# Hyena and attention step on one core: the filter spectrum's odd classes with three real products, the skip weight in the filter's first tap

## Chip, cores and metric

The kernel runs on one core of a Trainium2 chip. The metric is the device time of one execution in microseconds. Three runs of the kernel before took 884.54, 884.93 and 885.29 us; the median is 884.93 us. The engines are named as the profile names them: PE is TensorE (PEld its weight loads), DVE is VectorE, ACT is ScalarE, POOL is GpSimd, and SP issues most of the DMA transfers.

## The reference

One layer of a hybrid backbone works on 128 context tokens and 512 latent tokens, model width 1024. After an adaptive modulation one projection gives a gated long convolution (Hyena) and an attention with their gates; both are merged, projected, and normalised. The change touches the long convolution:

```python
def hyena_filters(L, ...):
    hf = jnp.sin(f_freq[0] * (z @ f_w1 + f_b1))
    hf = jnp.sin(f_freq[1] * (hf @ f_w2 + f_b2))
    hf = (hf @ f_w3).astype(jnp.float32).reshape(L, 2, D_HYENA)
    decay = jnp.exp(-t * jnp.abs(deltas)) + DECAY_SHIFT
    hf = hf * decay[:, None, :]
    return hf[:, 0], hf[:, 1]

def hyena_long_conv(v_h, x1, x0, h_fwd, h_bwd, d_bias):
    L = v_h.shape[1]
    u = v_h * x1
    filt_full = jnp.concatenate([h_fwd, jnp.zeros_like(h_fwd[:1]), h_bwd[:0:-1]], axis=0)
    n = 2 * L
    uf = jnp.fft.rfft(u.astype(jnp.float32), n=n, axis=1)
    ff = jnp.fft.rfft(filt_full, n=n, axis=0)
    y = jnp.fft.irfft(uf * ff[None], n=n, axis=1)[:, :L].astype(u.dtype)
    return (y + u * d_bias) * x0
```

The result of the convolution is then multiplied by `silu(g_h)` and goes into the merging projections.

## The kernel before

Channels lie on the 128 partitions, the 640 tokens on the free axis: 128 of the context, then 512 latent ones in blocks of 64 (8 grid rows by 8 columns, rolled by one block). Every large product is made of three matmuls: the operands are split into a high part (type fp32r, written by ACT) and a low part (the rest, written by DVE), and high x high, high x low and low x high are accumulated in PSUM. `split` (L100 to L102) makes such a pair, `mm3` (L155 to L158) the three matmuls, `accumulate` (L163 to L171) the projections.

The 1024 channels of the long convolution are worked through in four quarters of 256, two row tiles of 128 each. For each quarter these generators yield their work in steps:

- `quarter_head` projects the tiles of u and x1, runs the short convolution on them (`conv_tile`, L530) and multiplies them (L569).
- `quarter_tail` projects x0 and the gate g_h, and writes gate times x0 into a row tile yh (`gapped_product`, L523, which also brings the tokens from grid order into block order).
- `filter_spectrum` (L431) makes the filter's transform. The 512 latent taps are four time classes (every fourth tap, classes 0 to 3), the 128 context taps are class 4. For a class, `src` (L450) multiplies the hidden layer by the last filter weights (tile fl), takes the decay (sd, L459) and splits (sh, sl, L462). Its two halves of 256 columns are the sum and the difference of the forward and the backward filter. A shifted cosine and sine transform (tables dftH, dftL) follows per class, and the classes are combined into ten rows F of a quarter. Classes 1 and 3 go into the PSUM tiles fc and fd in eight groups of three matmuls (L488 to L493), for half of which the table of class 3 is negated (ndH, ndL, made at L413), and four 512-wide DVE operations combine them with the even classes (L497 to L500).
- L441 to L448 compute, with a matmul on the hidden layer's first column (fz), the backward filter's first tap, and subtract it from the skip weight: `hyd`.
- `long_conv` transforms u by the same tables (tiles ut, c_X, s_X, p_X) and multiplies it by F (L638 to L646). `long_conv_back` transforms back (yb), transposes (yp for the context, y for the latent tokens), adds u times hyd (L689, L698) and calls `gate_conv`, which multiplies the result into yh and sends yh to DRAM.

Tiles live in pools with a fixed number of buffers per tag; a tile waits for its buffer. PSUM has eight banks: four for the projections (tag mm, two per projection tile), four for all else (tag aux). `weave` (L68) mixes a main generator (projections) with a side generator (convolution and filter) in a fixed ratio, and `braid` (L706) alternates two side generators: while quarter q is transformed back, the filter of quarter q + 1 is made. In these stages (L724 to L729) only SP's early loads and a few table operations keep the written order; the other instructions are put into an order for each engine at build time, by a planner that follows the written order as its priority and simulates when each is ready (L1555). From the attention on (L1254), and in the prologue, PE's order is the written one.

The last quarter's convolution is woven with the first queries, keys and values (L1200); behind it `attention_setup` gives the convolution's memory to the attention.

Of the kernel before, what the change touches and what calls it, by code (L numbers as in the profile page):

```python
# [36 lines left out]
    (("convw", 96), ("hyd", 8), ("ident", 128)),  # L37
# [8 lines left out]
def tile_hyena_natten_step(ctx: ExitStack, tc: tile.TileContext, a, o):  # L46
# [3 lines left out]
    def f(ap):  # L50
        return ap.bitcast(F32)
# [181 lines left out]
    def hidden_layers():  # L233
        hf1 = temp("u", "hf1", 4)[:64]
# [19 lines left out]
    def prologue():  # L254
# [61 lines left out]
        for k in range(NK):  # L316
# [5 lines left out]
            row_ = hwa.tile([P, 2 * P], F32, tag="fb", bufs=2, name=f"row{k}")  # L322
# [13 lines left out]
            if k == 0:  # L336
                load_pack(1)
                out["zemb"] = temp("u", "zemb", 4)[:33]
# [53 lines left out]
    ndH = hyc.tile([P, 2, P], F32R, tag="ndH", name="ndH")  # L392
    ndL = hyc.tile([P, 2, P], F32R, tag="ndL", name="ndL")
# [9 lines left out]
    def dft_consts():  # L403
# [8 lines left out]
        for nd, src in ((ndH, dftH), (ndL, dftL)):  # L412
            nc.scalar.activation(nd[:], f(src[:, 0, 3]), AF.Copy, scale=-1.0)  # L413
# [17 lines left out]
    def filter_spectrum(q):  # L431
        if q not in pre:
            load_filter(q)
        w3 = pre[q]
        w3h = hwa.tile([P, 512], F32R, tag="w3h", name=f"w3h_{q}")
        w3l = hwa.tile([P, 512], F32R, tag="w3l", name=f"w3l_{q}")
        w3s = hwa.tile([P, 2, 256], F32, tag="fb", bufs=2, name=f"w3s_{q}")
# [3 lines left out]
        pb0 = aux(f"fz{q}")  # L441
        for i in range(2):
            nc.tensor.matmul(
                pb0[:, i : i + 1], w3[:, 256 + P * i : 384 + P * i], f(hid[:, 0:1]),
                start=True, stop=True, skip_group_check=True,
            )
# [3 lines left out]
        def src(cls):  # L450
# [7 lines left out]
            sd = hwa.tile([P, 2, 256], F32, tag="fb", bufs=2, name=f"sd{q}_{cls}")  # L458
            nc.vector.tensor_tensor(sd[:], two(ps[:]), dec[:].unsqueeze(1).to_broadcast([P, 2, 256]), op=ALU.mult)  # L459
            sh = hw.tile([P, 2, 256], F32R, tag="shl", bufs=4, name=f"sh{q}_{cls}")  # L460
            sl = hw.tile([P, 2, 256], F32R, tag="shl", bufs=4, name=f"sl{q}_{cls}")
            split(sh[:], sl[:], sd[:])  # L462
            return (sh[:, 0], sl[:, 0]), (sh[:, 1], sl[:, 1])

        s0 = src(0)
# [7 lines left out]
        s2 = src(2)  # L473
# [6 lines left out]
        pc = pd = None  # L480
        for cls in (1, 3):
            cs, ds = src(cls)
            yield
            first = cls == 1
            if first:
                pc = aux(f"fc{q}")
                pd = aux(f"fd{q}")
            for dst, i, (sh, sl), neg, lead in (  # L488
                (pc[:, :256], 0, cs, False, True), (pc[:, 256:], 1, ds, False, False),
                (pd[:, :256], 1, cs, not first, True), (pd[:, 256:], 0, ds, not first, False),  # L490
            ):
# [5 lines left out]
        nc.vector.tensor_tensor(x[:, 0:6:5], x[:, 1:7:5], two(pc[:]), op=ALU.add)  # L497
        nc.vector.tensor_tensor(x[:, 1:7:5], x[:, 1:7:5], two(pc[:]), op=ALU.subtract)
        nc.vector.tensor_tensor(x[:, 2:9:6], x[:, 3:8:4], two(pd[:]), op=ALU.add)
        nc.vector.tensor_tensor(x[:, 3:8:4], x[:, 3:8:4], two(pd[:]), op=ALU.subtract)  # L500
        yield
        pp = aux(f"fp{q}")
# [53 lines left out]
    def quarter_head(q):  # L556
        us = []
        out[f"u{q}"] = us
        for i in range(2):
            n = 2 * q + i  # L560
            u = hw.tile([P, NG + 1], F32, tag="u", bufs=4, name=f"u{n}")
# [11 lines left out]
    half_done = set()  # L573

    def gate_conv(n):
        if n in half_done:
            gapped_product(out["yh"][n], out[f"u{n // 2}"][n % 2])
            nc.sync.dma_start(yh_d[n], out["yh"][n][:])
        half_done.add(n)

    def quarter_tail(q):
        yh = out["yh"]
        for i in range(2):
# [7 lines left out]
            gate_conv(n)  # L591
# [57 lines left out]
    def long_conv_back(q):  # L649
        us, ident, hyd, R, W = out[f"u{q}"], out["ident"], out[f"hyd{q}"], out[f"R{q}"], out[f"W{q}"]  # L650
# [18 lines left out]
        for g, rs_ in enumerate(((0, 2), (1, 3), (4,))):  # L669
# [13 lines left out]
            yield  # L683
        outp = aux(f"yp{q}")
        for i in range(2):
            nc.tensor.transpose(outp[:, i * P : i * P + P], yp[:, i * P : i * P + P], ident)
        for i in range(2):
            up = us[i][:, :LP]
            nc.vector.scalar_tensor_tensor(  # L689
                up, up, hyd[:, i : i + 1], outp[:, i * P : i * P + P], op0=ALU.mult, op1=ALU.add  # L690
            )
        for i in range(2):
            n = 2 * q + i
            oy = aux(f"y{n}")
            for j, r in enumerate((0, 2, 1, 3)):
                nc.tensor.transpose(oy[:, r * P : r * P + P], ye[:, j, i * P : i * P + P], ident)
            uv = us[i][:, GAP:NG].rearrange("p (m r) -> p r m", r=4)
            nc.vector.scalar_tensor_tensor(  # L698
                uv, uv, hyd[:, i : i + 1], oy[:].rearrange("p (r m) -> p r m", r=4), op0=ALU.mult, op1=ALU.add
            )  # L700
            gate_conv(n)
# [728 lines left out]
def _host_constants():  # L1430
    f32 = np.float32
    zs, decs = [], []
    for L in (LS, LP):
# [7 lines left out]
        if L == LS:  # L1441
            zs += [z[r::4] for r in range(4)]
# [121 lines left out]
```

## Time and profile before

| | |
|---|---|
| median of three runs | 884.93 us (884.54 to 885.29) |
| span of the profiled execution, first to last instruction | 883.0 us |
| median of the runs less this span | 1.9 us |
| PE, PEld, DVE, ACT, POOL busy | 871.0, 843.5, 632.7, 429.5, 128.8 us |
| bytes moved | 129.07 MB, 146 GB/s |

The profile gives, of the profiled execution, the span alone; what lies around it is taken as the difference to the median of the runs. By stage: the prologue (modulation, first weights, hidden layers of the filter) runs to about 46 us, the four quarters of the long convolution with their projections to about 386 us, the attention with the remaining projections to about 705 us, the merging and output projections to the end. PE's rows name the tile that is written and the tiles that are read; a matmul's weight load has a row of its own under PEld. A row of a group ends with the busy time, the mean duration in ns, and the idle time of the engine just before; a row of the timeline begins with the start and the duration in us.

### The profile page before, as it was taken

To read this page: it belongs to the slowest core of one execution; us is meant where nothing else is said; L and a number is where in the kernel's file an instruction comes from. 1 tells how busy PE (TensorE), PEld (TensorE's weight loads), DVE (VectorE), ACT (ScalarE), POOL (GpSimd) and SP (SyncE) were. 2 spreads that over 40 slices of the span, in tenths; PEclk is the share of its full clock that TensorE was granted. 3 is DMA by queue.
4 is the path that set the end of the run, shared out by engine and by line. 5 is a ranking of instruction groups with operands and counts; after the bars stand their busy time and mean duration, and the time that the engine had idled before them with its cause. 6 is when DMAs were issued, how large, how long until landed. Compare 5 with 4: busy or idle time off the path is not lost.

```text
span 883.0 us, 16773 instructions
## 1 busy us (share of the span) xinstructions
PE 871.0 (99%) x6522; PEld 843.5 (96%) x6522; DVE 632.7 (72%) x1247; ACT 429.5 (49%) x919; POOL 128.8 (15%) x130
## 2 busy tenths in 40 slices
PE   8999999999999999999999999999999999999996
PEld 7899999999999999999999999999999999999885
DVE  5576693795668478699787567865788567676656
ACT  4486454655545432356665465555666632243200
POOL 1111010010101000024423222222222200000000
PEclk9999999999999999999999999999999999999999
DMA  9976666565656231253525153433252478545511
GB/s 325 401 164 148 134 136 126 132 140 118 168 112 142 70 108 55 72 195 105 164 80 169 55 152 100 142 105 122 80 181 83 132 285 283 181 152 198 214 64 55
DMA packets 54986, 129.07 MB, mean 146 GB/s; under 512 B 8283, under 2 KB 24283, under 8 KB 54908
## 3 DMA queue, kind: packets, MB, share of 16 engines
q1 hardware_dynamic: 45260, 107.62, 37.1%
q0 software_dynamic: 4032, 14.68, 10.2%
q10 hardware_dynamic: 5616, 5.70, 1.9%
q8 instruction: 51, 0.84, 0.4%
q14 instruction: 27, 0.22, 0.1%
HBM read 113.83 MB, written 14.16 MB: 145 GB/s over the span
## 4 chain that ended last, share of the span: by engine, by line
PE 96%; DMA 3%; DVE 1%; SPq 0%; issue 0%; DVEq 0%
PE mm L168 37%; PE sp L1125 23%; PE mm L182 6%; PE out L1391 6%; PE v L821 5%; PE pt L918 3%; PE s L925 2%; PE s L878 2%; DMA ada<-wada 2%; PE ve L833 1%; DMA xt<-xT 1%; PE yb L158 1%; PE yb L156 1%; PE fl L453 1%; PE yb L157 1%; PE ut L601 1%
## 5 line engine op out<-in xcount | busy, mean ns | idle before, releaser
L1125 PE MATMUL sp<-t,wb 128*128 128x320 f32 x768 | 120.6, 310 | 0.0
L1125 PEld LDWEIGHTS sp<-t,wb 128*128 128x128 f32 x768 | 113.8, 188 | 0.5 <-issue 0.5
L168 PE MATMUL mm<-hL,wh 128*128 128x320 f32 x480 | 113.8, 312 | 0.0
L168 PE MATMUL mm<-hH,wh 128*128 128x320 f32 x480 | 113.3, 312 | 0.3 <-ACT hH L365 0.3
L168 PE MATMUL mm<-hH,wl 128*128 128x320 f32 x480 | 111.4, 310 | 0.0
L1125 PE MATMUL sp<-hH,wb 128*128 128x320 f32 x384 | 93.2, 313 | 0.0
L168 PEld LDWEIGHTS mm<-hH,wh 128*128 128x128 f32 x480 | 80.5, 188 | 2.2 <-issue 1.2
L168 PEld LDWEIGHTS mm<-hL,wh 128*128 128x128 f32 x480 | 81.0, 188 | 1.2 <-DVE hL L373 0.4
L168 PEld LDWEIGHTS mm<-hH,wl 128*128 128x128 f32 x480 | 80.6, 188 | 0.3
L1125 PEld LDWEIGHTS sp<-hH,wb 128*128 128x128 f32 x384 | 66.1, 188 | 1.9 <-issue 1.9
L900 POOL TENSOR_SCALAR p<-p,sm 128x384 f32<-128x384 f32 x32 | 46.5, 1462 | 111.8 <-DVE sm L899 98.1
L101 ACT ACTIVATE wh<-raw 128x1024 fp32r<-128x1024 f32 x31 | 32.8, 1059 | 59.2 <-PE mm L168 23.8
L1125 PE MATMUL sp<-hL,wb 128*128 128x320 f32 x192 | 59.3, 309 | 0.0
L148 POOL DMA_DIRECT2D wl<-wall x28 | 24.3, 869 | 226.6 <-ACT wl L147 159.3
L102 DVE TENSOR_TENSOR wb<-s,wb 128x512 fp32r<-128x512 f32 x64 | 44.0, 701 | 15.8 <-ACT wb L101 15.7
L101 ACT ACTIVATE wb<-s 128x512 fp32r<-128x512 f32 x64 | 39.1, 629 | 27.7 <-DVE s L1090 21.5
L101 ACT ACTIVATE wb<-raw 128x512 fp32r<-128x512 f32 x48 | 30.1, 628 | 34.1 <-PE sp L1125 22.0
L102 DVE TENSOR_TENSOR wl<-raw,wh 128x1024 fp32r<-128x1024 f32 x31 | 37.9, 1221 | 12.0 <-ACT wh L101 11.9
L149 ACT ACTIVATE wh<-raw 128x1024 fp32r<-128x1024 f32 x28 | 29.7, 1060 | 33.1 <-PE mm L168 33.0
L1391 PE MATMUL out<-woh,yhs 128*128 128x512 f32 (+1 forms) x176 | 45.5, 372 | 0.0
L900 POOL TENSOR_SCALAR edge<-edge,sm 128x320 f32<-128x320 f32 x32 | 42.5, 1339 | 1.9 <-DVE sm L899 1.9
L168 PE MATMUL mm<-yhs,wh 128*128 128x320 f32 x224 | 41.9, 309 | 0.0
(364 smaller groups left out, 2160.5 us busy)
## 6 DMA issues: line engine op xcount, KB each, us to landing
raw<-wall SPq DMA_DIRECT2D x93, 512.0 KB, 3.6
wl<-wall POOLq DMA_DIRECT2D x28, 512.0 KB, 5.7
ada<-wada SPq DMA_DIRECT2D x16, 512.0 KB, 6.7
tm<-bias SPq DMA_DIRECT2D x16, 512.0 KB, 4.9
gate<-wgate SPq DMA_DIRECT2D x8, 512.0 KB, 4.0
wo<-wall SPq DMA_DIRECT2D x8, 512.0 KB, 4.5
xt<-xT SPq DMA_DIRECT2D x8, 320.0 KB, 7.0
dec<-decay SPq DMA_DIRECT2D x20, 128.0 KB, 5.1
```

What stands on the lines that cost most here:

```text
L101: hi = nc.scalar.activation(dst_h, src, AF.Copy)
L102: return hi, (eng or nc.vector).tensor_tensor(dst_l, src, f(dst_h), op=ALU.subtract)
L148: nc.gpsimd.dma_start(wl, a["wall"][i], accum_op=ALU.add)
L149: nc.scalar.activation(wh, raw[:], AF.Copy)
L168: nc.tensor.matmul(ps[hf][:, :HALF], wt[k], x[:, hf * HALF : (hf + 1) * HALF], start=(i == 0 and k == 0), stop=(i == lead[2] and k == NK - ...
L182: nc.tensor.matmul(p[:, :HALF], w[i // 2][k], (hH, hL)[i % 2][:, k, cs], start=n == 0, stop=n == len(steps) - 1, skip_group_check=True,)
L821: nc.tensor.matmul(ps[t // 2][:, t % 2 * 256 : t % 2 * 256 + 256], x[:, k, P * t : P * t + P], wk, start=first and t % 2 == 0, stop=last, ...
L878: nc.tensor.matmul(dst[h], x[rows(h), qs], y[rows(h), ks], start=i == 0, stop=i == 2, skip_group_check=True)
L900: nc.gpsimd.tensor_scalar_mul(pv, pv, sm[:, 2:3])
L918: nc.tensor.transpose(pt[:, i * P : i * P + P], x, ident)
L1125: nc.tensor.matmul(dst, wk, x(xi, k), start=j < 4 and k == 0 and i == 0, stop=k == 3 and i == 2, skip_group_check=True,)
L1391: ins = nc.tensor.matmul(dst, m[k][:, c0 : c0 + P], w[:, c : c + n], start=(first and k == 0), stop=(last and k == 5), skip_group_check=True,)
```

## The change

- **Class 3 reversed.** The host now lays out the hidden layer's input and the decay of time class 3 in reverse order. The reversed class's cosine transform is then, up to an alternating sign by frequency, the sine transform of class 1, and its sine transform the cosine of class 1. The two odd classes together have the form of a complex product, which is computed with three real products: the cosine of class 1 on the sum of both classes' taps (into fc, both column halves), and two tables, sine minus and sine plus cosine (`gs`, split into gsH and gsL), on the one and the other class. ACT copies the common product out of fc (tile t) before the second products are accumulated on it; DVE subtracts it from fd. The alternating sign is a per-partition factor (`sgn`), applied by `turn` where the rows of F are made: eight 256-wide DVE operations in place of four 512-wide ones. The negated tables go.
- **Skip weight.** hyd, the matmul on the first column and the additions of u times hyd go. A row `skip` (one partition, 256 columns) is loaded per quarter and brought into the first tap (partition 0) of classes 0 and 4 by three small DVE operations.
- **Gating.** `long_conv_back` multiplies the transposed result, read from PSUM, straight into yh: one operation for the context, three for the latent tokens, whose order is changed on the way. As yh must hold gate times x0 by then, the generator yields until `quarter_tail` has written it (`opened`); u is not needed after its transform, and has three buffers instead of four. The tag fb has three instead of two.

```diff
-    ndH = hyc.tile([P, 2, P], F32R, tag="ndH", name="ndH")
-    ndL = hyc.tile([P, 2, P], F32R, tag="ndL", name="ndL")
+    gsH = hyc.tile([P, 2, P], F32R, tag="gsH", name="gsH")
+    gsL = hyc.tile([P, 2, P], F32R, tag="gsL", name="gsL")
...
-        for nd, src in ((ndH, dftH), (ndL, dftL)):
-            nc.scalar.activation(nd[:], f(src[:, 0, 3]), AF.Copy, scale=-1.0)
+        gs = two(temp("e", "gs")[:, : 2 * P])
+        load_to(gs, two(a["gs"]))
+        split(gsH[:], gsL[:], gs)
...
+        skip = hwa.tile([1, 256], F32, tag="skip", name=f"skip{q}")
+        load_to(skip[:], a["hydr"][q : q + 1])
...
-        pb0 = aux(f"fz{q}")
-        for i in range(2):
-            nc.tensor.matmul(
-                pb0[:, i : i + 1], w3[:, 256 + P * i : 384 + P * i], f(hid[:, 0:1]),
-                start=True, stop=True, skip_group_check=True,
-            )
-        hyd = out[f"hyd{q}"] = const.tile([P, 2], F32, tag="hyd", bufs=2, name=f"hyd{q}")
-        nc.vector.scalar_tensor_tensor(hyd[:], pb0[:, :2], -DECAY0, out["hyd"][:, 2 * q : 2 * q + 2], op0=ALU.mult, op1=ALU.add)
...
+            if cls == 0:
+                nc.vector.scalar_tensor_tensor(skip[:], sd[0:1, 1], 0.5, skip[:], op0=ALU.mult, op1=ALU.add)
+            if cls in (0, 4):
+                nc.vector.scalar_tensor_tensor(sd[0:1, 0], sd[0:1, 0], 0.5, skip[:], op0=ALU.mult, op1=ALU.add)
+            return sd
...
-        for cls in (1, 3):
-            cs, ds = src(cls)
-            yield
...
-                lh, ll = (ndH[:, i], ndL[:, i]) if neg else (dftH[:, 0, cls, i], dftL[:, 0, cls, i])
-                mm3(dst, lh, ll, sh, sl, start=first and lead, stop=not first)
-            yield
-        s4 = src(4)
-        yield
-        nc.vector.tensor_tensor(x[:, 0:6:5], x[:, 1:7:5], two(pc[:]), op=ALU.add)
-        nc.vector.tensor_tensor(x[:, 1:7:5], x[:, 1:7:5], two(pc[:]), op=ALU.subtract)
-        nc.vector.tensor_tensor(x[:, 2:9:6], x[:, 3:8:4], two(pd[:]), op=ALU.add)
-        nc.vector.tensor_tensor(x[:, 3:8:4], x[:, 3:8:4], two(pd[:]), op=ALU.subtract)
-        yield
+        sd1 = taps(1)
+        yield
+        sd3 = taps(3)
+        t = spare("sd13_")
+        nc.vector.tensor_tensor(t[:], sd1[:], sd3[:], op=ALU.add)
+        sm = halves(13, t)
+        yield
+        pc = aux(f"fc{q}")
+        for i in range(2):
+            mm3(pc[:, 256 * i : 256 * i + 256], dftH[:, 0, 1, 0], dftL[:, 0, 1, 0], *sm[i], start=i == 0, stop=True)
+        nc.scalar.activation(t[:], two(pc[:]), AF.Copy)
+        s1 = halves(1, sd1)
+        yield
+        pd = aux(f"fd{q}")
+        mm3(pd[:, :256], gsH[:, 1], gsL[:, 1], *s1[0], stop=True)
+        mm3(pc[:, 256:], gsH[:, 0], gsL[:, 0], *s1[1], start=False)
+        s3 = halves(3, sd3)
+        yield
+        mm3(pc[:, :256], gsH[:, 0], gsL[:, 0], *s3[0], start=False)
+        mm3(pd[:, 256:], gsH[:, 1], gsL[:, 1], *s3[1], start=False)
+        s4 = halves(4, taps(4))
+        yield
+        sgn = out["sgn"]
+
+        def turn(dst, v, i, src):
+            nc.vector.scalar_tensor_tensor(x[:, dst], v, sgn[:, i : i + 1], x[:, src], op0=ALU.mult, op1=ALU.add)
+
+        nc.vector.tensor_tensor(t[:], two(pd[:]), t[:], op=ALU.subtract)
+        nc.vector.tensor_tensor(x[:, 0], x[:, 1], pc[:, :256], op=ALU.add)
+        nc.vector.tensor_tensor(x[:, 1], x[:, 1], pc[:, :256], op=ALU.subtract)
+        turn(5, pc[:, 256:], 0, 6)
+        turn(6, pc[:, 256:], 1, 6)
+        yield
+        turn(2, t[:, 0], 0, 3)
+        turn(3, t[:, 0], 1, 3)
+        nc.vector.tensor_tensor(x[:, 8], x[:, 7], t[:, 1], op=ALU.subtract)
+        nc.vector.tensor_tensor(x[:, 7], x[:, 7], t[:, 1], op=ALU.add)
...
-            gate_conv(n)
+            opened.add(n)
...
+        while 2 * q not in opened:
+            yield
         outp = aux(f"yp{q}")
...
-            up = us[i][:, :LP]
-            nc.vector.scalar_tensor_tensor(
-                up, up, hyd[:, i : i + 1], outp[:, i * P : i * P + P], op0=ALU.mult, op1=ALU.add
-            )
...
             n = 2 * q + i
+            while n not in opened:
+                yield
+            yh = out["yh"][n]
...
-            uv = us[i][:, GAP:NG].rearrange("p (m r) -> p r m", r=4)
-            nc.vector.scalar_tensor_tensor(
-                uv, uv, hyd[:, i : i + 1], oy[:].rearrange("p (r m) -> p r m", r=4), op0=ALU.mult, op1=ALU.add
-            )
-            gate_conv(n)
+            yp_ = yh[:, PC : PC + LP]
+            nc.vector.tensor_tensor(yp_, yp_, outp[:, i * P : i * P + P], op=ALU.mult)
+            ys = yh[:, SC : SC + LS].rearrange("p (b r d c) -> p r b d c", b=8, r=8, d=2)
+            yo = oy[:].rearrange("p (c r b d) -> p r b d c", c=4, r=8, b=8)
+            nc.vector.tensor_tensor(ys[:, :, 0], ys[:, :, 0], yo[:, :, 7], op=ALU.mult)
+            for d in range(2):
+                v = ys[:, :, 1:, d]
+                nc.vector.tensor_tensor(v, v, yo[:, :, :7, d], op=ALU.mult)
+            nc.sync.dma_start(yh_d[n], yh[:])
...
-            zs += [z[r::4] for r in range(4)]
-            decs += [dec[r::4] for r in range(4)]
+            zs += [z[r::4][:: -1 if r == 3 else 1] for r in range(4)]
+            decs += [dec[r::4][:: -1 if r == 3 else 1] for r in range(4)]
...
+    c1, s1 = dft[:, 0, 1, 0], dft[:, 0, 1, 1] * sgn
+    gs = np.concatenate([s1 - c1, s1 + c1], axis=1)
```

The buffer counts (tag u from 4 to 3, tag fb from 2 to 3) and the packed constants (hyd's eight columns make room for sgn's two) are left out of the diff.

More of the change, by code (lines that the diff above doesn't have):

```diff
@@ L457, in src, with halves @@
             dec = pre[q, cls]
-            sd = hwa.tile([P, 2, 256], F32, tag="fb", bufs=2, name=f"sd{q}_{cls}")
+            sd = spare(f"sd{cls}_")
             nc.vector.tensor_tensor(sd[:], two(ps[:]), dec[:].unsqueeze(1).to_broadcast([P, 2, 256]), op=ALU.mult)
-            sh = hw.tile([P, 2, 256], F32R, tag="shl", bufs=4, name=f"sh{q}_{cls}")
-            sl = hw.tile([P, 2, 256], F32R, tag="shl", bufs=4, name=f"sl{q}_{cls}")
+            if cls == 0:
[3 more added lines that the diff above has]
+            return sd
+        def halves(name, sd):
+            sh = hw.tile([P, 2, 256], F32R, tag="shl", bufs=4, name=f"sh{q}_{name}")
+            sl = hw.tile([P, 2, 256], F32R, tag="shl", bufs=4, name=f"sl{q}_{name}")
             split(sh[:], sl[:], sd[:])
-            return (sh[:, 0], sl[:, 0]), (sh[:, 1], sl[:, 1])
-        s0 = src(0)
+            return [(sh[:, i], sl[:, i]) for i in range(2)]
+        s0 = halves(0, taps(0))
         yield
@@ L472, in filter_spectrum @@
         yield
-        s2 = src(2)
+        s2 = halves(2, taps(2))
         yield
@@ L571, in quarter_head @@
             yield
[L573 to L579, printed above, removed]
+    opened = set()
     def quarter_tail(q):
@@ L649, in long_conv_back @@
     def long_conv_back(q):
-        us, ident, hyd, R, W = out[f"u{q}"], out["ident"], out[f"hyd{q}"], out[f"R{q}"], out[f"W{q}"]
+        ident, R, W = out["ident"], out[f"R{q}"], out[f"W{q}"]
         ab = hw.tile([P, 4, 256], F32, tag="plus", name=f"ab{q}")
```

31 lines of the change are left out of this document (12 added, 19 removed).

## The prediction

> **What bounds the kernel now.** I read the page first: busy time per engine, the span in slices, and the engines' shares of the chain that ended last.
>
> ```profile
> span 883.0 us, 16773 instructions
> PE 871.0 (99%) x6522; PEld 843.5 (96%) x6522; DVE 632.7 (72%) x1247; ACT 429.5 (49%) x919; POOL 128.8 (15%) x130
> PEclk9999999999999999999999999999999999999999
> PE 96%; DMA 3%; DVE 1%; SPq 0%; issue 0%; DVEq 0%
> ```
>
> TensorE is busy for 99% of the span and carries 96% of the chain, at full clock. The profile warns that a busy PE is not PE at its peak, since matmuls overlap, so I went on to the windows of 20 us, and there to single starts. Columns of the windows: length, then busy us and instruction count of PE, PEld, DVE, ACT, POOL, then granted clock, DMA share, GB/s.
>
> ```profile
> 20.00:40.00 20.00, 17.99 (x214) 15.30 (x214) 11.58 (x25) 8.82 (x19) 4.62 (x4) 1.00 1.03 404
> 100.00:120.00 20.00, 20.00 (x140) 19.82 (x139) 19.53 (x27) 10.75 (x18) 1.72 (x2) 1.00 0.67 143
> 180.00:200.00 20.00, 20.00 (x139) 19.82 (x139) 20.00 (x29) 9.11 (x16) 1.73 (x2) 1.00 0.68 140
> 200.00:220.00 20.00, 20.00 (x143) 19.91 (x143) 10.12 (x17) 11.12 (x22) 1.73 (x2) 1.00 0.54 117
> 260.00:280.00 20.00, 20.00 (x140) 19.91 (x139) 19.56 (x29) 8.04 (x15) 2.59 (x3) 1.00 0.73 158
> ```
>
> From 40 us on PE has no idle time in these windows. In the windows where the changed filter runs beside the long convolution (100, 180 and 260 us) VectorE is full as well: 19.5 to 20.0 of 20 us. So there are two candidates for a bound in this stage, and only one of them, PE, has no pause between these windows (DVE falls to 10.1 us at 200). The next rows, single PE instructions by start, show whether PE is dense inside "busy".
>
> ```profile
> 310.83 0.28 PE L157 MATMUL fc<-sl,dftH 128*128 128x256 f32 x1
> ...
> 312.02 0.31 PE L182 MATMUL mm<-hL,wh 128*128 128x320 f32 x1
> 705.18 91.51 PE mm L168 x624
> ```
>
> The first row is the first of ten filter matmuls of 256 columns in a row, the second the projection behind the tenth: (312.02 - 310.83) / 10 = 0.119 us each, though each lasts 0.28 us. The third row, from the chain, has 624 projection matmuls in 91.51 us, 0.147 us each. A matmul that is removed gives back its start-to-start time, not its duration.
>
> **The change on PE.** The odd time classes (1 and 3) of the filter spectrum took four products per channel pair and class, eight groups of three matmuls a quarter; now it is six groups (two for the common product, four for the rest): 24 matmuls become 18. The tap matmuls and the other classes' products keep their number, and so do the back transposes. The groups before:
>
> ```profile
> L156 PE MATMUL fc<-sh,dftH 128*128 128x256 f32 x16 | 4.7, 292 | 0.0
> L156 PE MATMUL fd<-sh,ndH 128*128 128x256 f32 x8 | 2.3, 283 | 0.0
> L443 PE MATMUL fz<-hid,w 128*128 128x1 f32 x16 | 2.0, 229 | 0.0
> ```
>
> Over four quarters 24 matmuls go: 24 x 0.119 = 2.86 us. The Trainium skill (TensorE: Matmul & The Clock Gate, Back-to-back issue gap) puts the gap of a warm isolated matmul at N/2.4 + 2.5 ns, which is 0.109 us for 256 columns, an estimate by which the term would be 2.62 us; the row's 0.119 us decides.
>
> The matmul on the first hidden column (fz), which took the backward first tap, goes too, two per quarter, each run as two (16 rows).
>
> ```profile
> 179.09 0.50 PE L443 MATMUL fz<-hid,w 128*128 128x1 f32 x4
> 179.46 0.54 PE L168 MATMUL mm<-hH,wl 128*128 128x320 f32 x2
> 179.84 0.46 PE L168 MATMUL mm<-hH,wh 128*128 128x320 f32 x2
> 256.60 0.50 PE L443 MATMUL fz<-hid,w 128*128 128x1 f32 x4
> 256.96 0.39 PE L168 MATMUL mm<-hL,wh 128*128 128x320 f32 x1
> ```
>
> Four of them hold PE 0.37 us (179.09 to 179.46), and the two projections behind take 0.38 us in place of 2 x 0.147, 0.09 more; the second place shows 0.36 for the four. That is 0.45 us a quarter, 1.8 us in all. PE work falls by 2.86 + 1.80 = 4.7 us.
>
> **On DVE.** The rows that price it (durations in ns; for L528 the smallest is the 64-wide form, the largest the 448-wide):
>
> ```profile
> L497 DVE TENSOR_TENSOR F<-F,fc 128x512 f32<-128x512 f32 x4 | 2.7, 686 | 0.2 <-PE fc L158 0.2
> L102 DVE TENSOR_TENSOR sl<-sd,sh 128x512 fp32r<-128x512 f32 x20 | 13.7, 687 | 9.5 <-ACT sh L101 5.7 <-PE mm L168 3.8
> L438 DVE TENSOR_TENSOR w3s<-w 128x256 f32<-128x256 f32 x4 | 1.7, 421 | 0.0
> L689 DVE SCALAR_TENSOR_TENSOR u<-u,hyd,yp 128x128 f32<-128x128 f32 x8 | 2.4, 341 | 0.0
> L698 DVE SCALAR_TENSOR_TENSOR u<-u,hyd,y 128x512 f32<-128x512 f32 x8 | 8.9, 1156 | 2.1 <-PE y L696 2.0
> L524 DVE TENSOR_TENSOR yh<-yh,u x8: 280/284/288, 149.4 to 378.9; 128x128 f32<-128x128 f32 x8
> L528 DVE TENSOR_TENSOR yh<-yh,u x16: 215/426/639, 154.5 to 379.9; 128x64 f32<-128x64 f32 x8, 128x448 f32<-128x448 f32 x8
> ```
>
> Filter, per quarter: four 512-wide combinations go (2.7 us, with the tiny skip operation 2.9). In come one more low half (0.69), the sum of two classes and the difference from the common product (0.69 each), eight 256-wide combinations (8 x 0.42 = 3.4) and three one-partition, 256-wide skip operations: no row has that form, and I take 0.42 each from the 256-wide row, since it is the width and not the partitions that they share; bounds 0.28 (128-wide row) and 0.69. Sum 6.7, so +3.8 us a quarter (3.4 to 4.6).
>
> Gating, per row tile: 0.34 + 1.16 + 0.28 + 0.22 + 0.64 = 2.6 us go (the skip additions with their stride-4 writes, then the gating pass). In come 0.28 for the prompt, 0.22 for the wrapped column block and two 224-wide products from PSUM in a four-index order, each between half of the 448 row (0.32) and 224/512 of the strided row (0.51); I take 0.5, because they read PSUM with a stride as that row does. Sum 1.5: -1.1 us a tile, -9 in all. DVE's total then moves by 4 x 3.8 - 9 = +6 us, to some 639 of 880: no bound as a total. In the full windows it is +3.8 us for the filter.
>
> **On ACT and in the queues.** ACT gets two 512-wide activations more a quarter (the high half of the class sum, and the copy of the common product), and trades the two negated tables for the high half of the new one.
>
> ```profile
> 68.46 0.65 ACT L101 ACTIVATE sh<-sd 128x512 fp32r<-128x512 f32 x1
> 69.80 0.62 ACT L471 ACTIVATE F<-fa 128x512 f32<-128x512 f32 x1
> 48.54 0.73 ACT L230 ACTIVATE hf<-arg 128x640 f32<-128x640 f32 x1
> 47.75 1.25 SPq L63 DMA_DIRECT2D raw<-wall  x2
> 56.16 0.33 SPq L63 DMA_DIRECT2D w<-fw  x1
> 85.35 9.98 SPq L63 DMA_DIRECT2D raw<-wall  x2
> SPq L63 <- DVE wl L102: 114.2, 24, 12.0
> ```
>
> That is 4 x 1.27 = 5 us on an engine that is 49% busy: nothing, with half of every window as cover. SP issues five DMAs more. The new table's load reuses the tile of the sine arguments, free once the sine at 48.54 has ended at 49.3; SP's next issue after 47.75 to 49.0 is at 56.16, so nothing is delayed behind it. The table is wanted only with the odd classes (the first at 74 us). Each skip row is 1 KB; it can stand on SP behind a weight load that waits, 9.98 us at 85 and 12.0 at the longest. Who waits for it is DVE at class 0, with all of DVE's queue behind that. I cost it at 0, because the load may be issued when the last quarter's class 4 is done, long before; without that lead it costs up to 12 us of DVE.
>
> **New waits on PE.** The second accumulation into the common product's bank must wait for ACT's copy of it (0.62 us plus ACT's queue), and the two differing products for the halves of class 1 and 3, which now queue behind the class sum: a chain longer by about one DVE and one ACT step, 3 us. PE's order has projections between these steps; and F is wanted late:
>
> ```profile
> 317.31 0.68 DVE L500 TENSOR_TENSOR F<-F,fd 128x512 f32<-128x512 f32 x1
> 339.93 1.49 DVE L638 TENSOR_TENSOR W<-X,F 128x1280 f32<-128x1280 f32 x1 [0.34 <-ACT X L630]
> 379.12 1.42 DVE L528 TENSOR_TENSOR yh<-yh,u 128x64 f32<-128x64 f32 x4
> POOL edge L864 <- DVE yh L528: 95.9, 1, 95.9
> 386.19 1.50 PE s L878 x16
> ```
>
> In the last quarter the odd classes are combined by 318.0 and used at 339.9: 22 us of slack. At the end of the stage the attention's tiles wait for the last gating (380.5), 5.7 us before the first scores; the gating becomes shorter and no longer holds the convolution's inputs, so this hand-over gets easier. I cost the new waits at 0 and bound them: below by 0 (no stall is there now that could vanish), above by the 0.62 us copy and one low half, 0.69, twice a quarter, 4 x 2.6 = 10 us, if nothing lay between.
>
> **Sum.** 883.0 - 4.7 = 878.3 us of span. The page gives only the span; the runs' median, 884.9, stands 1.9 us above it, and I carry that: **880.3 us**, -0.5%. The runs spread from 884.54 to 885.29, so 0.2% (1.8 us) is about what can be told from no change.
>
> **Rivals.**
> *DVE takes over in the full windows (slower).* For: DVE has 0 to 0.5 us to spare in 20 us at 100, 180 and 260, and gets 3.8 us more there. It decides if DVE falls so far behind that a projection's accumulator isn't emptied when PE wants it back: a tile is 48 matmuls, 48 x 0.147 = 7 us, and two tiles' banks rotate, so a lag of over 7 us. Against: DVE has 9.9 us free in the following window, and 3.8 is under 7. If the whole of it reached PE in the three woven quarters: 884.9 - 4.7 + 11.4 = 891.6. The Trainium skill (TensorE: Matmul & The Clock Gate, The HAM clock gate) says that an idle window of about 3.4 us halves the PE clock for the next, and a DVE lag is what would make such a gap; the estimate is 1.7 us more per gap. The trace shows no loss of clock even where PE pauses (1.00 at 20 to 40 us), and no run here shows such a gap.
> *The gain is eaten (no change).* The order of instructions is laid out anew, and the common product's copy, or the bank of the prompt's back transposes, which is now held until both row tiles are gated, makes PE wait about 1.2 us a quarter: 4.8 of the 4.7 us are gone, 885.0. For: four such banks exist and two hold the odd classes meanwhile. Against: PE lost nothing at the present dependencies of the same kind (idle 0.0 in the fc, fd and fz rows).
> *Only the products count.* If fz's place were filled by another switch of matmul kinds, 2.9 us remain: 882.1.
>
> **How the numbers follow.** Forecast 0.68 (879 to 882 is its own range), products only 0.11, eaten 0.09, DVE takes over 0.12. So faster 0.79, within 0.2% 0.09, slower 0.12. The range reaches from 878.5 (the forecast and a gain of 1.8 us that I don't see) to 886.0, past the eaten case; the slower case is left out.
>
> **What would show it.** The groups of fc and fd together with 72 matmuls in place of 96, no fz rows; the span 4 to 5 us shorter, and the first scores at 381 to 382 us instead of 386.2, the distance from there to the end unchanged. L698's successor well under 1.16 us, DVE's total 4 to 8 us up. Wrong would be: idle time on PE ahead of fc or fd ended by ACT's copy, projection groups (L168, L182) with starts over 0.147 us apart behind DVE, or a DVE wait on the skip row's DMA.

## The result, and the profile after

The changed kernel takes 889.89 us (median of five runs, 887.90 to 890.05), the kernel before on the same chip 884.66 (884.54 to 885.29). The ratio is 1.005, with an interval of 1.0038 to 1.0062: it is slower by half a per cent, where 880.3 us and a gain of half a per cent had been forecast. The profiled execution took 887.9 us, 1.8 around its span.

The page of the kernel after: span and busy time by engine.

```profile
span 886.1 us, 16753 instructions
PE 867.8 (98%) x6482; PEld 839.4 (95%) x6482; DVE 636.7 (72%) x1276; ACT 433.5 (49%) x926; POOL 128.3 (14%) x130
```

PE has 40 instructions fewer (24 filter matmuls and the 16 fz rows), DVE is busy 4.0 us longer (632.7 before) and ACT 4.0 (429.5): the change does what it says. Yet the span is 3.1 us longer. The windows of the kernel after (columns as in the prediction) show where:

```profile
100.00:120.00 20.00, 17.39 (x120) 17.01 (x120) 16.34 (x22) 9.70 (x17) 1.72 (x2) 1.00 0.53 112
180.00:200.00 20.00, 16.36 (x100) 15.51 (x99) 18.51 (x24) 9.69 (x20) 0.86 (x1) 0.91 0.32 69
260.00:280.00 20.00, 19.94 (x138) 19.53 (x137) 18.71 (x25) 12.49 (x24) 1.86 (x3) 1.00 0.59 126
```

Before, PE was busy for 20.00 of 20 us in each of these. Now it pauses in the first two, and in the second its clock drops to 0.91. The waits of PE in the kernel after name the release (total us, times, longest):

```profile
PE mm L168 <- DVE yh L569: 5.2, 2, 2.6
PE p_X L157 <- DVE ul L102: 1.1, 1, 1.1
```

PE's timeline after, the rows on both sides of each pause and the matmuls behind the last one (start us, duration us; the idle time in brackets):

```profile
108.99 0.28 PE L158 MATMUL p_X<-uh,dftL 128*128 128x256 f32 x1
111.88 0.42 PE L168 MATMUL mm<-hH,wh 128*128 128x320 f32 x1 [2.61 <-DVE yh L569]
...
183.66 0.40 PE L453 MATMUL fl<-w3l,hid 128*128 128x512 f32 x1
185.16 0.38 PE L157 MATMUL p_X<-ul,dftH 128*128 128x256 f32 x1 [1.10 <-DVE ul L102]
...
185.74 0.28 PE L158 MATMUL p_X<-uh,dftL 128*128 128x256 f32 x1
188.56 0.42 PE L168 MATMUL mm<-hH,wh 128*128 128x320 f32 x1 [2.54 <-DVE yh L569]
...
189.63 0.47 PE L168 MATMUL mm<-hH,wh 128*128 128x320 f32 x1
189.90 0.47 PE L168 MATMUL mm<-hL,wh 128*128 128x320 f32 x1
```

From start to start, less the normal spacing, the pauses cost 2.8 us (108.99 to 111.88), 1.3 and 2.7 us. Behind the last one the starts are 0.267 us apart in place of 0.147, from 189.6 to 193.0 us: 13 matmuls, 1.6 us. Sum 8.4 us lost against 4.7 us of work that went, a balance of +3.7. The first scores of the attention confirm it (PE's timeline after):

```profile
389.80 0.33 PE L898 MATMUL s<-k,q 64*128 64x128 f32 x2
```

and of the kernel before:

```profile
386.12 0.33 PE L878 MATMUL s<-k,q 64*128 64x128 f32 x2
```

They start 3.7 us later (the prediction's 386.19 is from the chain, whose group begins a little behind this row), and from there to the end it is 496.3 us against 496.9. All of the loss lies in the long convolution's quarters. (The profiled execution was the fastest of the five. The other four took 889.0 to 890.05, 1.1 to 2.2 us more, with mean clocks of 0.992 to 0.994 against 0.996. One more slow stretch like the one at 189.6 us would cost 1.6 us and take 0.002 off the mean clock (3.4 of 886 us at 0.52); that is an estimate, and no profile of theirs shows where they lost it.)

**What is late.** The chain behind the first pause, from the timelines of PE, ACT and DVE after, ordered by time:

```profile
101.27 0.38 PE L617 MATMUL ut<-pack,u 128*128 128x128 f32 x2
...
101.57 0.92 ACT L562 ACTIVATE u<-zs,pack 128x641 f32<-128x641 f32 x1 [0.44 <-PE ut L617]
...
104.71 0.88 DVE L564 SCALAR_TENSOR_TENSOR u<-zs,pack,u 128x641 f32<-128x641 f32 x1
...
108.24 0.88 DVE L564 SCALAR_TENSOR_TENSOR u<-zs,pack,u 128x641 f32<-128x641 f32 x1
...
110.79 0.77 ACT L574 ACTIVATE yh<-mm 128x320 f32<-128x320 f32 x2
...
111.34 0.88 DVE L569 SCALAR_TENSOR_TENSOR yh<-yh,mm 128x320 f32<-128x320 f32 x2 [0.88 <-ACT yh L574]
...
112.86 0.29 ACT L556 ACTIVATE zs<-mm 128x128 f32<-128x128 f32 x1
```

The first row is the last transpose of this quarter's u. The second row is the first step of a short convolution for the next quarter, and it *writes* a tile u. With three buffers that tile's buffer is the one that the transpose has just read; with four it was another. So the step can't come before the transpose, and the staging tile zs that it reads (one of two) is held until the two further steps on DVE, at 104.7 and 108.2, have ended (109.1). The next projection, x0's, was complete at 99 us (the gate's 48 matmuls follow it), but needs this zs: it leaves PSUM only at 112.86. PE finishes the gate's projection at 108.5 with both pairs of banks full, and must wait until the gate is out, which ACT and DVE do at 110.8 to 111.9 (1.28 us of ACT's time ahead of it is a table load, which the kernel before has at this place too). The view of the transpose tiles in the kernel after tells who waited for them (us, times):

```profile
  ACT u L562: 5.0, 2
```

The kernel before has no such entry. There the same step ran at 86.91 us, 9.5 us ahead of its quarter's last transposes (96.4); from ACT's timeline before:

```profile
86.91 0.94 ACT L541 ACTIVATE u<-zs,pack 128x641 f32<-128x641 f32 x1
```

The wait itself is short at the first place (0.44 us) because the planner had put the step late in ACT's order; it is the lateness that is passed on. At the second place ACT stood for 4.57 us. PE's wait of 1.1 us there is for a split (ul) that DVE does at 184.69 us, late in the same way.

### The profile page after: what moved, and what is told of

The parts are those of the page before. It is cut to its first block, busy times and chain, and to the rows that moved or that the text cites. A ratio compares the mean times of both kernels' runs of the same rounds, so it can differ in the third digit from the quotient of the medians.

```text
span 886.1 us, 16753 instructions
## 1 busy us (share of the span) xinstructions
PE 867.8 (98%) x6482; PEld 839.4 (95%) x6482; DVE 636.7 (72%) x1276; ACT 433.5 (49%) x926; POOL 128.3 (14%) x130
## 4 chain that ended last, share of the span: by engine, by line
PE 95%; DVE 2%; DMA 2%; ACT 0%; issue 0%; POOL 0%; DVEq 0%; POOLq 0%
PE mm L168 37%; PE sp L1145 23%; PE out L1411 6%; PE mm L182 6%; PE v L841 5%; PE pt L938 3%; PE s L945 2%; PE s L898 2%; DMA ada<-wada 2%; PE ve L853 1%; PE adaT L249 1%; PE yb L157 1%; PE yb L158 1%; PE yb L156 1%; PE adaT L266 1%; PE fl L452 0%
## 5 line engine op out<-in xcount | busy, mean ns | idle before, releaser
L168 PE MATMUL mm<-hH,wh 128*128 128x320 f32 x480 | 118.8, 314 | 5.5 <-DVE yh L569 5.2
L168 PE MATMUL mm<-hL,wh 128*128 128x320 f32 x480 | 117.4, 312 | 0.0
L168 PE MATMUL mm<-hH,wl 128*128 128x320 f32 x480 | 116.7, 311 | 0.0
L168 PEld LDWEIGHTS mm<-hH,wl 128*128 128x128 f32 x480 | 82.4, 189 | 0.4
```

Of the source, the lines that this page charges most:

```text
L168: nc.tensor.matmul(ps[hf][:, :HALF], wt[k], x[:, hf * HALF : (hf + 1) * HALF], start=(i == 0 and k == 0), stop=(i == lead[2] and k == NK - ...
```

## Experiments

The question was whether PE's pauses come from u having three buffers in place of four (theory A), from the work that DVE gets (theory B, the rival of the prediction), or from the longer chain of the odd classes (theory C). After e1 to e4 came theory D: the gating, which now yields until yh is there, holds back the filter's last steps. Times are medians of four to eleven runs, beside the kernel before on the same chip (884.88 us beside e1 to e4, 884.95 to 884.97 beside the others). The planner lays out every kernel's order anew, so each run also compares two orders.

### e1: the fourth buffer given back

```diff
-            mod = const.tile([P, 2, 2], F32, tag="mod", bufs=4, name=f"mod{k}")
+            mod = const.tile([P, 2, 2], F32, tag="mod", bufs=3, name=f"mod{k}")
...
-        pre[q] = hwa.tile([P, 512], F32, tag="sd", bufs=2, name=f"w3_{q}")
+        pre[q] = hwa.tile([P, 512], F32, tag="sd", bufs=1, name=f"w3_{q}")
...
-            u = hw.tile([P, NG + 1], F32, tag="u", bufs=3, name=f"u{n}")
+            u = hw.tile([P, NG + 1], F32, tag="u", bufs=4, name=f"u{n}")
```

The first two edits make room for the last (a prologue tile and the raw filter weights lose a buffer).

> The changed kernel with four buffers for u again (room is made by one buffer for the raw filter weights and three for the modulation). Theory A, the third-buffer theory: ACT's first tap of u for the second row tile of the next quarter waits until the last transposes of this quarter's u (101.57 us behind the transpose at 101.27, 181.96 behind 181.66), keeps its staging tile zs, so the next projection is not emptied, and PE waits for a bank. Without it PE has no wait from 60 to 380 us and the gain comes out: 884.7 - 4.7 = 880 us (879 to 881.5). Theory B, VectorE is overrun by the filter's 3.8 us more a quarter: the waits stay, 887 to 890. Theory C, the longer chain of the odd classes keeps the auxiliary banks and delays the convolution: waits stay but move, 884 to 889.

Measured: 882.91 us (882.36 to 884.91), ratio 0.9979 (0.9970 to 0.9987). The pauses in the quarters are gone: PE has no wait from 60 to 320 us. That is 7.0 us under the kernel after. But 880 wasn't reached, and the time lies in no theory's range. Two waits of PE are new against the kernel after, both at 320 to 325 us:

```profile
PE fp L156 <- ACT sh L101: 1.7, 1, 1.7
...
PE v L841 <- DVE ql L785: 0.4, 1, 0.4
```

The steps behind the first, from the timelines of DVE, ACT and PE of this kernel:

```profile
317.95 2.51 PE L182 MATMUL mm<-hH,wl 128*128 128x320 f32 x16
...
321.43 0.63 ACT L101 ACTIVATE sh<-sd 128x512 fp32r<-128x512 f32 x1 [2.22 <-DVE sd L462]
322.11 0.39 PE L156 MATMUL fp<-sh,dftH 128*128 128x256 f32 x1 [1.65 <-ACT sh L101]
322.82 0.89 ACT L783 ACTIVATE q<-mm 128x128 fp32r<-128x128 f32 x4 [0.76 <-DVE sl L102]
```

At the hand-over to the attention the projections on PE have run out of banks (the queries are taken from theirs only at 322.8, behind the filter's high half in ACT's order), and the next thing in PE's order is the last step of the last filter, which isn't ready. Theory A explains 7.0 us of the miss, and 2.6 us are left to the forecast.

### e5: the control for the room

Only the room-making edits of the experiment before, with u's three buffers kept.

> The changed kernel with three u buffers and only the room-making of the four-buffer run (one buffer for the raw filter weights, three for the modulation). If the fourth u buffer made that run faster, this one stays slow, with a wait on PE in the woven quarters: 886 to 890. If the room-making itself moved the order of instructions to a luckier one, it comes near 883.

Measured: 889.84 us (889.31 to 890.52), ratio 1.0055 (1.0043 to 1.0068), and PE's wait for yh again 5.2 us in two places. The 7 us are the buffer's, not those of the room made for it.

### e2: three buffers, claimed later

```diff
+            v = hwa.tile([P, NG + 1], F32, tag="cv", bufs=2, name=f"v_{n}") if i else u
-            tiles = ((n, u), (8 + n, x1))
+            tiles = ((n, v), (8 + n, x1))
...
-            nc.vector.tensor_tensor(u[:, :NG], u[:, :NG], x1[:, :NG], op=ALU.mult)
+            nc.vector.tensor_tensor(u[:, :NG], v[:, :NG], x1[:, :NG], op=ALU.mult)
```

The second row tile's short convolution goes into a tile of another tag, and u is claimed only by the product with x1, on DVE.

> The changed kernel with three buffers for u, but the second row tile's short convolution goes into a tile of the tag cv, and a u buffer is claimed only by the product with x1, some 8 to 15 us later. Theory A: the wait on the transposes falls behind work that is done by then, PE's waits of 2.6 and 3.6 us go, 880 to 882 us; if the two cv buffers now turn over too slowly, a wait of ACT on cv takes their place, up to 885. Theory B and C: nothing is changed for VectorE or the banks, 887 to 890.

Measured: 885.84 us (885.01 to 889.50), ratio 1.0016 (1.0007 to 1.0025), between the ranges of the theories. The pauses from 60 to 300 us are gone here too. The wait for the transposes is still there, but it is now one of DVE, of its product of the second row tile (the view of the transpose tiles, us and times):

```profile
  DVE u L591: 4.0, 2
```

So it isn't the number of buffers by itself but the moment of the claim, and that it stops ACT, which PE felt. The hand-over is worse: 6.5 us of lost PE time from 316 to 328, the largest row again the wait for the last filter step (2.3 us).

### e3: the three products alone

The kernel before with the reversed class, the tables gs and `turn`, but with hyd, fz and the old gating, u with four buffers.

> The three products alone on the kernel before: skip weight, first-column matmuls, gating and four u buffers as before (one buffer for the raw filter weights). Theory A: PE loses 24 x 0.119 = 2.9 us and waits for nothing: 881.8 us (881 to 883). Theory B: VectorE has its 3.8 us more a quarter less the skip operations, and the longer gating too, so this is the worst case for it: 888 or more. Theory C: the longer chain is all in here, 885 to 888.

Measured: 883.54 us (882.59 to 886.26), ratio 0.9982 (0.9972 to 0.9992). The page and PE's waits of this kernel:

```profile
PE 868.4 (99%) x6498; PEld 840.6 (95%) x6498; DVE 644.0 (73%) x1276; ACT 432.1 (49%) x926; POOL 125.6 (14%) x130
```
```profile
PE sp L1148 <- DVE wb L102: 1.4, 1, 1.4
...
PE fp L157 <- DVE sl L102: 0.5, 1, 0.5
```

DVE has more work than in any other kernel here (644.0 us), and from 60 to 380 us PE loses only 0.8 us, once, at 163. That speaks against theory B, and against C for the pauses. The time is half a us above theory A's range: the products gain 1.3 us, and 2.4 us of PE's time are lost on the two rows shown (0.8 at 163 and 1.6 at 416, from start to start). The second lies in the attention, and why it appears there these runs don't show.

### e4 and e6: the skip weight and the gating alone, with three and with four buffers

Four products as before; fz and hyd out, skip and `opened` in. The first run has three buffers for u, the second four and one for the raw filter weights. Against the kernel before, in short:

```diff
-        pb0 = aux(f"fz{q}")
...
+        skip = hwa.tile([1, 256], F32, tag="skip", name=f"skip{q}")
+        load_to(skip[:], a["hydr"][q : q + 1])
...
-            gate_conv(n)
+            opened.add(n)
```

> The other part alone on the kernel before: skip weight in the first tap, gating from PSUM, three u buffers; the four products as before. Theory A: the wait is in here: the last transposes of u come at 96.7 us in the kernel before, u's first tap at 86.9, so ACT waits up to 10 us and PE waits for a bank unless the rest of the stage gives it room: between 883 (room) and 888. Theory B: VectorE has less to do (-1.1 us a row tile, +1.2 us skip operations a quarter), PE loses 1.8 us: 882.9 (882 to 883.5). Theory C: the chain is short, 882.9.

> Skip weight in the first tap and gating from PSUM alone, with four u buffers; the four products as before. Theory A, the u buffer is what made this part slow with three (888.4): PE loses 1.8 us, 883 us, up to 884.5 with a wait at the hand-over to the last quarter's values. Theory D, the gating that waits for gate times x0 holds back the filter's last steps, so that the filter is late at the hand-over whatever the buffers: 885 to 888, with PE idle at 315 to 330 us.

Measured: with three buffers 888.36 us (888.21 to 889.62), ratio 1.0046 (1.0032 to 1.0060), just above theory A's range; with four 883.06 (882.51 to 883.36), ratio 0.9977 (0.9967 to 0.9987), without a wait of PE from 60 to 380 us. The gain with four, 884.97 - 883.06 = 1.9 us, is the fz term of the prediction (1.8). Having three buffers in place of four costs 5.3 us here, without the three products: most of it (3.9 us) at 320 to 330, in several waits, the largest again that for the last filter step (1.3 us). The second run has the gating that yields and no wait at the hand-over, against theory D's range of 885 to 888: with four buffers the yielding alone does no harm. The wait of the first experiment takes the longer chain of the odd classes as well.

### e7: the gating behind the weave, with four buffers

The transposes and the gating become a generator of their own, which runs when its quarter's projections are written; nothing yields for `opened`. u has four buffers, as in the first experiment.

```diff
-        while 2 * q not in opened:
-            yield
+        out[f"back{q}"] = ye, yp
+
+    def gate_back(q):
+        ident, (ye, yp) = out["ident"], out[f"back{q}"]
...
-            while n not in opened:
-                yield
...
+        now(gate_back(q))
...
-    weave(hand_over(), chain(long_conv(3), long_conv_back(3), attention_setup()), 6 * NK + N_VALUES, N_CONV + N_BACK + 1)
+    weave(hand_over(), chain(long_conv(3), long_conv_back(3), gate_back(3), attention_setup()), 6 * NK + N_VALUES, N_CONV + N_BACK + 1)
```

> The changed kernel with four u buffers, and the last part of the back transform (transposes and gating) moved behind the weave of its quarter, so that it no longer yields in turn with the filter's last steps until gate times x0 is there. Theory D: PE's wait of 1.7 us before fp and 0.6 behind it at 320 to 324 us go, 880 to 881.5. If the late filter comes from its own longer chain (theory C), the wait stays: 882.5 to 884.

Measured: 880.02 us (879.81 to 880.73), ratio 0.9944 (0.9932 to 0.9957): faster than both kernels. The page, its windows at the places of the pauses and at the hand-over, and the first scores:

```profile
span 878.2 us, 16752 instructions
PE 866.2 (99%) x6482; PEld 838.7 (95%) x6482; DVE 637.5 (73%) x1276; ACT 432.3 (49%) x926; POOL 129.2 (15%) x130
```
```profile
100.00:120.00 20.00, 20.00 (x141) 19.92 (x140) 16.54 (x25) 11.32 (x22) 2.36 (x3) 1.00 0.58 134
180.00:200.00 20.00, 20.00 (x140) 19.83 (x140) 16.94 (x25) 10.39 (x20) 2.47 (x3) 1.00 0.59 136
260.00:280.00 20.00, 20.00 (x139) 19.83 (x138) 20.00 (x29) 11.53 (x22) 2.59 (x3) 1.00 0.61 143
320.00:340.00 20.00, 20.00 (x167) 20.00 (x166) 14.25 (x22) 6.55 (x17) 0.00 (x0) 1.00 0.23 74
```
```profile
381.63 0.33 PE L899 MATMUL s<-k,q 64*128 64x128 f32 x2
```

From 60 us to the first scores PE loses nothing, and the span is 4.8 us shorter than before, the 4.7 us of PE work that the change removes. At 260 us DVE is busy for 20.00 of 20 us, and PE still doesn't wait: a full DVE alone doesn't stop it. The last filter's chain ends earlier than in the first experiment. The rows of the filter's last step, of this kernel and then of the first experiment's (durations in ns, first and last start):

```profile
L156 PE MATMUL fp<-sh,dftH x8: 283/284/286, 90.9 to 315.5; 128*128 128x256 f32 x8
```
```profile
L156 PE MATMUL fp<-sh,dftH x8: 278/282/386, 91.1 to 323.5; 128*128 128x256 f32 x8
```

It is 8 us earlier at the hand-over. That the yielding steps took the filter's turns in `braid` is how the code reads; the runs show only that the lateness goes with them.

### e8, e9 and e10: the gating behind the weave, with three buffers

The same move, with u's three buffers; then with the later claim of the third experiment; then for the skip weight and gating alone.

> The same move with three u buffers. Theory A: the wait on the transposes of u stays, PE idles 2 to 4 us in at least one woven quarter, 885 to 890. Theory D, if it were the whole cause: 880 to 882.

> The kernel of the late claim (three u buffers, the second row tile's u claimed by the product) with the gating behind the weave. Theory D: its waits of 6.5 us at 316 to 328 us were those of the filter held back by the gating, and go: 880 to 881.5. If the wait on the u buffer, moved to VectorE's product, holds back the side work as well, waits stay in the woven quarters or at the hand-over: 882 to 886.

> Skip weight and gating alone, with three u buffers, and the gating behind the weave; four products, so the filter's chain is the short one. If the third buffer hurts by itself, without the longer chain and without the gating that yields (theory A in its strict form): slower than the same part with four buffers (883.1), 884.5 to 889, with PE waits. If three buffers hurt only together with one of the other two: 882.5 to 883.5.

Measured, in this order: 890.79 us (888.98 to 894.68), ratio 1.0057 (1.0044 to 1.0071); 880.51 (880.31 to 883.40), ratio 0.9955 (0.9943 to 0.9968); 893.07 (892.05 to 894.34), ratio 1.0091 (1.0076 to 1.0107). PE's waits in the first of the three (its profiled execution was the slowest of the five, 894.68):

```profile
PE mm L168 <- DVE yh L569: 6.0, 2, 3.3
...
PE mm L168 <- ACT zs L559: 2.3, 1, 2.3
```

With the move alone the full change stays slow, just above theory A's range, and the release is the same as in the kernel after; the second row is the staging tile itself. With the late claim three buffers are nearly as good as four (880.51 against 880.02): DVE waits for the transposes 5.7 us in three places, and PE waits for none of it in the quarters; it loses 0.9 us at the hand-over and 0.8 in the attention. The full change, by buffers and gating:

| median us | gating yields | gating behind the weave |
|---|---|---|
| three buffers | 889.89 | 890.79 |
| three, second tile claimed late | 885.84 | 880.51 |
| four buffers | 882.91 | 880.02 |

The last of the three runs is only partly understood. It is 4 us slower than the upper end of its range. ACT's first step on u waits 3.1 us for the transposes, as theory A has it, and PE loses 4.5 us at 180 to 200, a stretch at a lower clock included. But some 4.5 us more are lost at 380 to 440, in the attention, and no run here tells why.

## Why the prediction was wrong

- **PE's work: right.** fc and fd have 72 matmuls in place of 96, the fz rows are gone. Where PE waits for nothing new the span falls by 4.8 us against the 4.7 of the sum, and the first scores stand at 381.63 us, inside the forecast 381 to 382. The fz part alone measured 1.9 against 1.8. The products alone came to 1.3 us, with 2.4 of waits in them, against 2.86; the two make 3.7, and where the 0.9 too much comes from isn't shown. The rival "only the products count" (882.1) is refuted by the fz part.
- **DVE and ACT: right in total, and not the bound.** DVE +4.0 us by the page (+6 forecast), ACT +4.0 (+5). The rows of the kernel after, and one of the first experiment's gating, show the sizes:

```profile
89.32 0.47 DVE L511 SCALAR_TENSOR_TENSOR F<-fc,pack,F 128x256 f32<-128x256 f32 x1
...
112.14 0.41 DVE L460 SCALAR_TENSOR_TENSOR skip<-sd,skip 1x256 f32<-1x256 f32 x1
```
```profile
314.79 0.68 DVE L720 TENSOR_TENSOR yh<-yh,y 128x224 f32<-128x224 f32 x2
```

  The skip operations cost 0.41 (0.42 taken), `turn` 0.47 (0.42), a 224-wide gating product 0.34 (0.5 taken; the lower bound, 0.32, was the nearer row). The skip row's load delayed nothing.
- **The step that failed: "I cost the new waits at 0".** The bound of 10 us would have held the 8.4 us lost, but it was built from the wrong waits: the copy of the common product and the class sum, ahead of fc and fd. The profile after has no PE wait on either, nor on the bank of the prompt's transposes, which the rival "the gain is eaten" named (one wait on the copy, 0.5 us, stands in e2). The wait that came is on a tile whose buffer count the change lowers. The prediction took the shorter life of u as an easing ("no longer holds the convolution's inputs") and never asked who writes the next u, and when. Before, that write ran 9.5 us ahead of the last transposes. With one buffer less it can only come behind them, and ACT, DVE, the staging tile and PE's banks hang on it in a row.
- **The chain's length: too short.** "Longer by about one DVE and one ACT step, 3 us": the first quarter's fp starts at 90.3 us in place of 81.0, 9 us later, and with it the first transposes of u (90.4 in place of 81.2) and the last (101.3 in place of 96.4). That made the wait on the transposes longer. It isn't enough alone: with four buffers the same fp stands at 90.9 us (gating behind the weave) and costs nothing.
- **The hand-over: the slack was counted to the wrong reader.** "22 us of slack" ran from the combination of the odd classes to the product with F at 339.9. But the filter's last transform (fp) stands in PE's order ahead of other work, and PE came to it 1.65 us early once the quarters ran without a pause. The filter had gained nothing meanwhile: the last of these starts stands at 323.3 us in the kernel before and at 323.5 in the first experiment, and the work that PE no longer had was the time by which it came too soon. In the kernel after this is hidden behind the pauses: its window from 320 to 340 us is full.
- **The rival "DVE takes over": right release, near time, wrong mechanism.** 891.6 was worked out from DVE's work, and PE does wait for a DVE row (yh). At the first pause DVE had stood idle for 0.88 us right ahead of that row, waiting for ACT's gate. At the second it ran without a gap from 181.49 us, and the gate's row came behind all of that. These are the steps there, first in the kernel after, then in the first experiment (ACT and DVE):

```profile
181.49 0.69 DVE L638 TENSOR_TENSOR pl_X<-e_X,c_X 128x512 f32<-128x512 f32 x1 [3.59 <-PE c_X L158]
...
184.06 0.74 ACT L574 ACTIVATE yh<-mm 128x320 f32<-128x320 f32 x2
...
188.03 0.87 DVE L569 SCALAR_TENSOR_TENSOR yh<-yh,mm 128x320 f32<-128x320 f32 x2
```
```profile
179.95 0.75 ACT L574 ACTIVATE yh<-mm 128x320 f32<-128x320 f32 x2
...
180.41 0.89 DVE L569 SCALAR_TENSOR_TENSOR yh<-yh,mm 128x320 f32<-128x320 f32 x2 [1.85 <-ACT yh L574]
...
182.08 0.68 DVE L638 TENSOR_TENSOR pl_X<-e_X,c_X 128x512 f32<-128x512 f32 x1
```

  With four buffers DVE's same run of additions begins even later, but the gate is through before it, since ACT isn't stopped for the transposes. With three, ACT stood until 181.96 and took the gate only at 184.06, when DVE had the additions in hand. The kernel with 644.0 us of DVE work, and the one with DVE full at 260 us, speak against the rival's mechanism as well.
- **The clock.** The windows of the kernel after around its second pair of pauses show the drop:

```profile
184.00:188.60 4.60, 0.96 (x7) 0.70 (x6) 4.60 (x9) 2.35 (x5) 0.86 (x1) 1.00 0.62 139
189.60:193.00 3.40, 3.40 (x15) 3.40 (x15) 3.40 (x5) 1.82 (x5) 0.00 (x0) 0.52 0.45 105
```

  With PE busy for 0.96 of 4.60 us the granted clock is 0.52 for the next 3.4 us, which cost the 1.6 us worked out above. The single pause of 2.8 us at 109 cost no clock in this profile. But a single pause can: in e8 one of the same idle time, 2.61 us, ends at 114.85 us, and from 115.9 to 119.1 the starts are again 0.267 us apart. Its window has PE busy for the same 17.39 us as that of the kernel after, at a clock of 0.91 in place of 1.00:

```profile
100.00:120.00 20.00, 17.39 (x112) 17.09 (x111) 14.22 (x23) 11.48 (x20) 1.73 (x2) 0.91 0.48 105
```

  The Trainium skill (TensorE: Matmul & The Clock Gate, The HAM clock gate) says that an idle window of some 3.4 us halves the clock until a busy one has passed. The length of the slow stretch agrees, and so does the price that the rival put on it (1.7 us). The idle time ahead of it doesn't: PE's longest idle time ahead of these two stretches was 2.54 and 2.61 us, so less was enough.

## What to carry to other kernels

When a change takes a buffer from a tag, price it as a wait: find the instruction that writes the next tile of that tag, the last reader of the tile whose buffer it gets, and whether the first still comes behind the second; then follow everything that stands behind that writer on its engine. Slack of a late result is counted to the first instruction that must wait for it and holds up others behind it in its engine's order, not to the reader of the final product. A bound on "new waits" is worth only as much as the list of waits it is built from: make the list from the tags and buffers in the diff, not only from its new instructions.

## What the runs showed of the hardware

A pause of PE can cost more than its length, and its length alone doesn't tell: two pauses within 5 us (1.3 and 2.7) were followed by 3.4 us at a clock of 0.52 and 1.6 us of loss; after a single one of 2.61 us idle the clock fell in e8 and didn't fall in the kernel after. What decides between the two these runs don't show. And an engine that is busy for all of a 20-us window (DVE, 260 to 280 us in the fastest kernel) held up nothing, while at 18.5 of 20 (180 to 200 us in the kernel after) the row that PE waited for stood behind its other work: what counts is the order of its work, not its share.
